# Ten mixer units of a two-layer hybrid step, worked in a different order

## The chip, the cores and the metric

The kernel runs on one core of one Trainium2 chip. The metric is device time in microseconds (us), as the median of the runs shown. One further execution was recorded by the hardware profiler, and every row below comes from it. Engine names: PE is TensorE (matmuls and transposes), PEld its weight loads, DVE is VectorE, ACT is ScalarE, POOL is GpSimd, and SP is SyncE, which issues every transfer of this kernel in one queue.

## What is computed

Two layers, each over 640 tokens: 512 latent ones and 128 prompt ones, with a model width of 1024. Cut to what matters here, a layer is:

```python
h = rmsnorm(x, g_norm1) * (1 + m[1]) + m[0]
z = h @ w_in                       # q, k, v of three mixers, and three gates
oa = diff_attention(qa, ka, va)    # (softmax(q1 k1) - lam softmax(q2 k2)) v, then a per-head norm
ob = gqa_attention(qb, kb, vb)     # q and k normalised per head and rotated first
oc = neighbourhood_attention(...)  # a window of the grid plus context, with a bias
x = x + m[2] * (sum(gate_i * (o_i @ w_branch_i)) @ w_out)
x = x + m[5] * (relu(rmsnorm(x, g_norm2) ... @ w1) ** 2 @ w2)
```

The latent tokens read their own keys and 128 cached context keys. The prompt tokens read only their own keys, and their keys and values are outputs too.

## The kernel before

The program is recorded as a list of operations, each with its engine, its operands and an estimated length. A planner (`Plan.schedule`) then goes through the list and decides, engine by engine, the order in which the operations are issued: whenever an engine is free it takes, among the operations that are ready by its estimate, the one with the lowest place in the list (moved a little by `EVAC` and `FILL`, one number for each kind of unit). So the order in which the program is written is a priority, and the order on each engine is fixed before the run. On the chip each engine works through its own fixed order and waits wherever the next operation isn't ready.

A layer's first stage, the mixers, is cut into `NU = 10` units of 384 columns of `w_in`. `kind(u)` gives the kind: units 0 to 3 are differential (A, one head pair each), 4 and 5 are grouped-query (B, four query heads each), and 6 to 9 are neighbourhood (C, two heads each). In this text A2 or B5 means the kind and the unit's number. The loop over the units, L1307, does three things for each:

- `project` (L924): for each of five tiles of 128 tokens, 24 matmuls of 128x384 into one of two PSUM banks. The weight blocks come from a stream (`ws`), in the order in which the host has packed them (`_stream`, L1571); each is split by ACT and POOL into a high and a low part ahead of use. There is room for ten blocks, and one unit needs eight.
- `evacuate` (L932), per tile: for A, DVE and POOL rotate q and k. For B there is a chain ahead of that: ACT squares, DVE sums, POOL takes the power -1/2 (a tensor_tensor on 128x5), and DVE scales five heads (five operations on 128x64). For C nothing is rotated. Then all kinds are split into high and low parts, transposed by PE through a single bank, and copied out.
- `jobs` (L1095): the attention itself. A has one job, B five (four heads and the prompt), C three. A job has two or three stages: scores, maximum, exponential and row scaling; then transposes of the rows and the product with v; for A also a norm over the head and a store. `step(i)` (L1300) writes one stage of each of three jobs into the list, so a unit's attention stands in the list just behind its projection and ahead of the next unit's. A row is 640 wide in A and B and 384 wide in C, and POOL scales it (L305).

The unit's number also picks its buffers: two places each for q, k and the prompt's k, three for v (L856). After the ten units come the gates and branch products, the output projection and the MLP. Those begin with gate products that need none of the mixers' outputs, so PE can take them while the last jobs run; each writes two of six PSUM banks.

Of the kernel before, what the change touches and what calls it, by code (L numbers as in the profile page):

```python
# [25 lines left out]
NU = 10  # L26
# [16 lines left out]
PRE = 2  # L43
LAG = 3
ORDER = (0, 1, 4, 2, 3)
LAM_INIT = [0.8 - 0.6 * math.exp(-0.3 * l) for l in range(DEPTH)]


# [9 lines left out]
class Plan:  # L58
# [16 lines left out]
    def __init__(self, nc):  # L75
        self.nc = nc
        self.ops = []
        self.writer = {}
        self.readers = {}
        self.bias = 0  # L80
        self.views = {}
# [380 lines left out]
def hybrid_plan(pl, a, mf, mr, view, psm, xspill, ospill):  # L462
# [44 lines left out]
    class Banks:  # L507
        def __init__(self, ids, w=1):
            self.ids, self.w, self.i = ids, w, 0
# [311 lines left out]
    def kind(u):  # L821
        return "A" if u < 4 else ("B" if u < 6 else "C")
# [29 lines left out]
            self.kp = [u1b[:, 1536:1792], u1b[:, 1792:2048]]  # L852

    class Unit:
        def __init__(self, l, u, ph):
            self.l, self.u, self.k, self.p = l, u, kind(u), ph  # L856
            q, kk, v, kp = ph.q[u % 2], ph.kk[u % 2], ph.v[u % 3], ph.kp[u % 2]
            self.kp = kp.rearrange("p (h k) -> p h k", h=2)
            self.qall = q.rearrange("p (f t) -> p f t", f=4)
            if self.k == "B":  # L860
                self.q = self.qall
                self.kk = kk.rearrange("p (h k) -> p h k", h=2)
                self.v = v[:, :6 * P].rearrange("p (c d) -> p c d", c=6)
            elif self.k == "A":
                self.q = q.rearrange("p (h s t) -> p h s t", h=2, s=2)
                self.kk = kk.rearrange("p (h k) -> p h k", h=2)
                self.v = v.rearrange("p (c s d) -> p c s d", c=6, s=2)
            else:
                self.q = q.rearrange("p (h s t) -> p h s t", h=2, s=2)
                self.kk = kk.rearrange("p (h k) -> p h k", h=2)  # L870
                self.v = v.rearrange("p (c h d) -> p c h d", c=6, h=2)
# [228 lines left out]
        def job_A(self):  # L1100
# [43 lines left out]
            pl.ptt(ssum, ssum, mhalf[:, :5], ALU.pow)  # L1144
            pl.pts(ssum, ssum, 1.0 - LAM_INIT[l], 0.0, ALU.mult, ALU.add)
            tt(on, on, ssum.unsqueeze(2).to_broadcast([P, 5, P]), ALU.mult)
# [130 lines left out]
    first = first_norm(Turns([u0[:, i * D:(i + 1) * D] for i in range(6)] + [wms.get(), wms.get()]), Bump(u1, 0, UNIT1A), u1c[:, :D])  # L1277
    first_z = {t: psm[:, b, :UW] for t, b in zip(ORDER, (2, 0, 1, 3, 7))}
    W = []
    for k in first:  # L1280
        W.append(ws.get(UW, 1))
        for t in ORDER:
            Unit.summand(None, first_z[t], W, t, k)
# [7 lines left out]
    for l in range(DEPTH):  # L1291
        ts(nlam[:, l:l + 1], nlam[:, l:l + 1], 1.0, -LAM_INIT[l], ALU.mult, ALU.add)

    for l in range(DEPTH):
        last = l == DEPTH - 1
        ph = Phase1()
# [7 lines left out]
                    next(jobs[j], None)  # L1304

        n = 0
        for u in range(NU):  # L1307
            un = Unit(l, u, ph)
            un.cached()
            if l == 0 and u == 0:  # L1310
                for t in ORDER:
                    un.evacuate(first_z[t], t)
            else:
                ws.hold = ws.cur
                W = [ws.get(UW, 1) for _ in range(KT)]
                ws.hold = None
                for t in ORDER:
                    un.project(W, t)
            for job in un.jobs():
                jobs.append(job)  # L1320
                step(n)
                n += 1
# [247 lines left out]
def _stream(i):  # L1570
    parts, pairs = [], []  # L1571
    for l in range(DEPTH):
        w_in = i["w_in"][l]
        for u in range(NU):
            parts.append(_kmajor(w_in[:, _unit_cols(u)], 0, UW))
        for b, n in enumerate(("w_branch_a", "w_branch_b", "w_branch_c")):
            for d in range(KT):
# [26 lines left out]
    out, at, np_ = [], 0, 0  # L1604
# [113 lines left out]
```

## Time and profile before

| what | value |
|---|---|
| median of 3 runs (lowest, highest) | 2405.42 us (2403.06, 2407.76) |
| profiled execution: its time | 2407.02 us |
| profiled execution: its span | 2405.1 us |
| mean granted TensorE clock | 0.989 |
| PE busy, weight loads busy | 2331.6 us (97%), 2262.4 us (94%) |
| DVE busy | 1825.6 us (76%) |
| ACT busy | 1215.3 us (51%) |
| POOL busy | 447.9 us (19%) |
| transfers | 245.39 MB, mean 102 GB/s |

The span runs from the first to the last instruction; 1.9 us of the profiled execution's time lie around it. Busy time counts an engine's own instructions, so an engine that waits isn't busy. The two layers have their mixers at about 84 to 500 us and 1215 to 1665 us of the span.

### The profile page before, as it was taken

The page shows a single profiled execution, that of the slowest core. Times are in us where ns is not written, and L with a number is a line of the kernel's source. Part 1 is how long each engine was busy: PE and PEld are TensorE (multiplying, and loading weights), DVE is VectorE, ACT ScalarE, POOL GpSimd, SP SyncE. Part 2 cuts the span into 40 slices and gives each one's busy share as a digit, 9 for nine tenths or more (in the row PEclk, how much of TensorE's full clock was granted, in tenths as well). Part 3 has the DMA queues.
Part 4 walks back from the last instruction along what each step waited for, and adds up shares of the span by engine and source line. Part 5 has one row for each costly group of instructions (what it writes and reads, how often), then busy time and mean ns, then how long its engine had stood idle before and what let it go on. Part 6 is the DMA issues. An engine that isn't in the chain of part 4 may idle for free. (4 is left out here: it accounts for less than half of the span.)

```text
span 2405.1 us, 42038 instructions
## 1 busy us (share of the span) xinstructions
PE 2331.6 (97%) x15484; PEld 2262.4 (94%) x15484; DVE 1825.6 (76%) x4002; ACT 1215.3 (51%) x2826; POOL 447.9 (19%) x528
## 2 busy tenths in 40 slices
PE   7899999999999999999999999999999999999997
PEld 5898999999999999999989998999999999999997
DVE  6878778789836999877777887777983677777776
ACT  4556677642232735444476567765232363544442
POOL 4535533310000000000034455431000000000000
PEclk8999999999999999999999999999999999999998
DMA  6211112476422244332241112136662222223322
GB/s 243 84 49 59 58 44 68 137 238 213 151 79 65 77 140 132 106 85 79 77 130 51 57 48 61 56 104 219 203 214 74 83 59 73 81 80 84 82 73 67
DMA packets 104754, 245.39 MB, mean 102 GB/s; under 512 B 12770, under 2 KB 24546, under 8 KB 103524
## 3 DMA queue, kind: packets, MB, share of 16 engines
q1 hardware_dynamic: 104548, 242.71, 32.9%
q8 instruction: 122, 2.00, 0.4%
q14 instruction: 84, 0.69, 0.1%
HBM read 225.62 MB, written 17.04 MB: 101 GB/s over the span
## 5 line engine op out<-in xcount | busy, mean ns | idle before, releaser
L245 PE MATMUL psm<-mr 128*128 128x384 f32 (+2 forms) x10784 | 1807.1, 319 | 20.1 <-ACT mr L262 8.1
L245 PEld LDWEIGHTS psm<-mr 128*128 128x128 f32 x10784 | 1657.8, 189 | 29.7 <-ACT mr L262 10.2
L262 ACT ACTIVATE mr<-mf 128x384 fp32r<-128x384 f32 (+4 forms) x956 | 471.5, 515 | 675.3 <-PE psm L245 589.1
L267 DVE TENSOR_TENSOR mr<-mf,mr 128x384 fp32r<-128x384 f32 (+5 forms) x795 | 438.4, 564 | 170.8 <-ACT mr L262 165.7
L311 POOL TENSOR_TENSOR mf<-mf 128x256 f32<-128x256 f32 (+3 forms) x93 | 90.4, 973 | 1236.0 <-DVE mf L267 1215.9
L280 DVE SCALAR_TENSOR_TENSOR mf<-psm,mf 128x256 f32<-128x256 f32 (+2 forms) x580 | 209.8, 407 | 107.2 <-PE psm L245 97.6
L262 ACT ACTIVATE mf<-mf 128x320 f32<-128x320 f32 (+6 forms) x409 | 191.9, 491 | 100.5 <-DVE mf L267 48.1
L305 POOL TENSOR_SCALAR mf<-mf 128x640 f32<-128x640 f32 (+3 forms) x236 | 145.4, 620 | 353.0 <-DVE mf L267 289.8
L294 DVE CUSTOM_DVE_ANT_0 psm<-mf,U1B 128x1024 f32<-128x1024 f32 x160 | 198.4, 1240 | 10.4 <-DMA mf<-wmod 9.5
L311 POOL TENSOR_TENSOR mr<-mf,mr 128x384 fp32r<-128x384 f32 (+1 forms) x169 | 189.4, 1142 | 55.1 <-ACT mr L262 54.4
L262 ACT ACTIVATE mf<-psm,mf 128x640 f32<-128x640 f32 (+3 forms) x256 | 162.6, 643 | 65.7 <-DVE mf L267 48.3
L267 DVE TENSOR_REDUCE mf<-psm 128x1 f32<-128x640 f32 (+2 forms) x212 | 148.4, 704 | 39.1 <-PE psm L245 33.5
L245 PE MATMUL psm<-U,mr 128*128 128x320 f32 (+1 forms) x1110 | 174.9, 305 | 0.6 <-ACT mr L262 0.5
L245 PEld LDWEIGHTS psm<-U,mr 128*128 128x128 f32 x1110 | 163.7, 189 | 1.2 <-ACT mr L262 0.6
L267 DVE TENSOR_TENSOR mr<-psm,mr 128x512 fp32r<-128x512 f32 (+2 forms) x252 | 141.1, 579 | 24.5 <-ACT mr L262 22.0
L245 PE MATMUL psm<-U1A,mr 128*128 128x256 f32 (+2 forms) x814 | 152.9, 309 | 0.0
L262 ACT ACTIVATE mr<-psm 128x512 fp32r<-128x512 f32 (+2 forms) x252 | 123.7, 513 | 53.5 <-PE psm L248 45.9
L267 DVE TENSOR_TENSOR mf<-mf 128x320 f32<-128x320 f32 (+8 forms) x261 | 134.2, 522 | 8.5 <-POOL mf L305 5.9
L245 PEld LDWEIGHTS psm<-U1A,mr 128*128 128x128 f32 x814 | 132.2, 188 | 0.0
L267 DVE TENSOR_TENSOR mf<-psm,mf 128x128 f32<-128x128 f32 (+5 forms) x248 | 93.0, 391 | 43.8 <-ACT mf L262 23.4
L248 PE MATMUL psm<-mf 128*128 128x128 f32 x752 | 120.2, 276 | 4.6 <-DVE mr L267 2.6
L262 ACT ACTIVATE mf<-psm 128x320 f32<-128x320 f32 (+7 forms) x188 | 76.3, 410 | 75.1 <-PE psm L245 71.0
(95 smaller groups left out, 1714.4 us busy)
## 6 DMA issues: line engine op xcount, KB each, us to landing
mf<-w SPq DMA_DIRECT2D x232, 384.0 KB, 3.2
mf<-wmod SPq DMA_DIRECT2D x84, 512.0 KB, 3.8
mf<-w SPq DMA_DIRECT2D x156, 256.0 KB, 2.7
U1C<-w SPq DMA_DIRECT2D x48, 256.0 KB, 2.7
mf<-bias SPq DMA_DIRECT2D x8, 1024.0 KB, 5.4
U<-wmod SPq DMA_DIRECT2D x12, 512.0 KB, 6.1
mf<-x SPq DMA_DIRECT2D x16, 320.0 KB, 7.0
ospill<-mf SPq DMA_DIRECT2D x16, 256.0 KB, 2.6
```

The costliest lines, as they stand in the source:

```text
L245: self.add("PE", d, lambda R: self.nc.tensor.matmul(R(out), R(lhsT), R(rhs), start=start, stop=stop), [out], [lhsT, rhs])
L248: self.add("PE", 55 if in_.dtype == F32R else 108, lambda R: self.nc.tensor.transpose(R(out), R(in_), ident), [out], [in_, ident])
L262: self.add("ACT", d, lambda R: self.nc.scalar.activation(R(out), R(in_), func, **kw), outs, ins)
L267: self.add("DVE", d, lambda R: getattr(self.nc.vector, name)(R(out), *map(R, ins), *args, **kw), [out] + list(extra), list(ins) + [x for x ...
L280: self.add("DVE", d, lambda R: self.nc.vector.scalar_tensor_tensor(R(out), R(a), s, R(b), op0, op1), [out], [a, b] + ([s] if hasattr(s, "a ...
L294: self.add("DVE", d, lambda R: self.nc.vector.tensor_tensor_reduce(out=R(out), in0=R(a), in1=R(b), scale=1.0, scalar=0.0, op0=ALU.mult, op ...
L305: self.add("POOL", d, lambda R: self.nc.gpsimd.tensor_scalar(R(out), R(a), s1, s2, op0, op1), [out], [a] + [s for s in (s1, s2) if hasattr ...
L311: self.add("POOL", d, lambda R: self.nc.gpsimd.tensor_tensor(R(out), R(a), R(b), op), [out], [a, b])
```

## The change

The loop over the units, and the host code that packs the weight stream, take the units in the order of a new table: A0, C6, A1, B4, C7, A2, C8, B5, A3, C9 in place of A0 to A3, B4, B5, C6 to C9. A unit's buffers are picked by its place in that order and no longer by its number. No operation is added or removed, and no size changes.

```diff
@@ -43,6 +43,7 @@
 ORDER = (0, 1, 4, 2, 3)
+UNITS = (0, 6, 1, 4, 7, 2, 8, 5, 3, 9)
@@ -852,9 +853,9 @@
     class Unit:
-        def __init__(self, l, u, ph):
+        def __init__(self, l, u, ph, n):
             self.l, self.u, self.k, self.p = l, u, kind(u), ph
-            q, kk, v, kp = ph.q[u % 2], ph.kk[u % 2], ph.v[u % 3], ph.kp[u % 2]
+            q, kk, v, kp = ph.q[n % 2], ph.kk[n % 2], ph.v[n % 3], ph.kp[n % 2]
@@ -1304,8 +1305,8 @@
         n = 0
-        for u in range(NU):
-            un = Unit(l, u, ph)
+        for at, u in enumerate(UNITS):
+            un = Unit(l, u, ph, at)
             un.cached()
@@ -1571,7 +1572,7 @@
         w_in = i["w_in"][l]
-        for u in range(NU):
+        for u in UNITS:
             parts.append(_kmajor(w_in[:, _unit_cols(u)], 0, UW))
```

The planner then issues the same operations in another order on every engine. Three places follow, all in the first layer; source lines are one higher after the change.

DVE, the third tile of B5's evacuation. The rows on 128x64 are its five head scalings; 128x512 on `mr` is the low part of a job's transposed rows, TENSOR_REDUCE from `psm` to 128x1 is a row maximum of a job. Before:

```order
L280 SCALAR_TENSOR_TENSOR mf<-psm,mf 128x64 x2
L267 TENSOR_TENSOR mr<-psm,mr 128x512 x2
L267 TENSOR_REDUCE mf<-psm 128x1
L280 SCALAR_TENSOR_TENSOR mf<-psm,mf 128x64
L267 TENSOR_TENSOR mr<-psm,mr 128x512
L267 CAST U1C_93_650<-psm 128x2x128
L267 RECIPROCAL mf<-mf 128x1
L280 SCALAR_TENSOR_TENSOR mf<-psm,mf 128x64 x2
```

After:

```order
L281 SCALAR_TENSOR_TENSOR mf<-psm,mf 128x64 x4
L268 TENSOR_TENSOR mf<-psm,mf 128x128
L281 SCALAR_TENSOR_TENSOR mf<-psm,mf 128x64
L268 CAST U1C_93_648<-psm 128x2x128
L268 TENSOR_TENSOR mr<-mf,mr 128x4x64
L268 TENSOR_TENSOR U_4_78_510<-mf,U_4_78_510 128x128
L268 TENSOR_REDUCE mf<-mf 128x5
L268 TENSOR_TENSOR mr<-mf,mr 128x128
```

Before, the five scalings stood in three pieces, with maxima and splits of B4's and A3's jobs between them. After, they stand in two pieces, and what follows are copies and splits of evacuations, of A2's job and of A3's cached keys.

POOL, beside a grouped unit's evacuation. TENSOR_TENSOR 128x5 is the power -1/2, with a TENSOR_SCALAR 128x5 ahead of it; `mr` 128x384 is the low part of a weight block of the next unit; TENSOR_SCALAR 128x640 scales a row of an A or B job, and 128x384 a row of a C job. Before, B4's evacuation, while B5's weights are made ready:

```order
L305 TENSOR_SCALAR mf<-mf 128x640
L311 TENSOR_TENSOR mr<-mf,mr 128x384 x4
L311 TENSOR_TENSOR mf<-mf 128x320
L305 TENSOR_SCALAR mf<-mf 128x640
L305 TENSOR_SCALAR mf<-mf 128x5
L311 TENSOR_TENSOR mr<-mf,mr 128x384
L311 TENSOR_TENSOR mf<-mf 128x5
L311 TENSOR_TENSOR mr<-mf,mr 128x384
L305 TENSOR_SCALAR mf<-mf 128x128
L311 TENSOR_TENSOR mr<-mf,mr 128x384
L305 TENSOR_SCALAR mf<-mf 128x5
L311 TENSOR_TENSOR mf<-mf 128x5
```

After, B5's evacuation, while A3's weights are made ready:

```order
L306 TENSOR_SCALAR mf<-mf 128x384
L306 TENSOR_SCALAR mf<-mf 128x5
L312 TENSOR_TENSOR mf<-mf 128x5
L306 TENSOR_SCALAR mf<-mf 128x5
L312 TENSOR_TENSOR mr<-mf,mr 128x384
L306 TENSOR_SCALAR mf<-mf 128x5
L312 TENSOR_TENSOR mr<-mf,mr 128x384
L312 TENSOR_TENSOR mf<-mf 128x5
L306 TENSOR_SCALAR mf<-mf 128x384
L312 TENSOR_TENSOR mr<-mf,mr 128x384 x2
L306 TENSOR_SCALAR mf<-mf 128x5
L312 TENSOR_TENSOR mr<-mf,mr 128x384
```

Weight blocks stand between the powers in both. The rows scaled there were 640 wide, of A3, and are 384 wide, of C8; behind the piece before came the evacuation of a second grouped unit, and behind the piece after comes a differential one.

POOL, the end of the mixer stage. Before, with C8 and C9 last:

```order
L305 TENSOR_SCALAR mf<-mf 128x384 x2
L311 TENSOR_TENSOR mr<-mf,mr 128x384 x6
L305 TENSOR_SCALAR mf<-mf 128x384
L311 TENSOR_TENSOR mr<-mf,mr 128x384
L305 TENSOR_SCALAR mf<-mf 128x384 x2
L305 TENSOR_SCALAR mf<-mf 128x128 x2
L305 TENSOR_SCALAR mf<-mf 128x384 x5
L305 TENSOR_SCALAR mf<-mf 128x128 x2
L305 TENSOR_SCALAR mf<-mf 128x384 x8
```

After, with B5, A3 and C9 last (128x256 is the rotation of A3's last tile, the 128x5 rows are A3's norm over its head):

```order
L312 TENSOR_TENSOR mf<-mf 128x256
L312 TENSOR_TENSOR mr<-mf,mr 128x384
L306 TENSOR_SCALAR mf<-mf 128x640 x11
L306 TENSOR_SCALAR mf<-mf 128x128
L306 TENSOR_SCALAR mf<-mf 128x384 x6
L306 TENSOR_SCALAR mf<-mf 128x5
L312 TENSOR_TENSOR mf<-mf 128x5
L306 TENSOR_SCALAR mf<-mf 128x5
L306 TENSOR_SCALAR mf<-mf 128x384
L306 TENSOR_SCALAR mf<-mf 128x128 x2
L306 TENSOR_SCALAR mf<-mf 128x384
```

Before, the last rows are those of two neighbourhood units. After, eleven rows of 640 columns of B5 and A3 stand there behind the last weight block, and A3's norm stands among C9's rows.

## Rows read from the trace of the kernel before

**Rows 1.** The page: busy time, share of the span and instructions of each engine; and TensorE's granted clock in the 40 slices of the span, in tenths.

```profile
PE 2331.6 (97%) x15484; PEld 2262.4 (94%) x15484; DVE 1825.6 (76%) x4002; ACT 1215.3 (51%) x2826; POOL 447.9 (19%) x528
...
PEclk8999999999999999999999999999999999999998
```

**Rows 2.** Busy time of each engine in four long stretches: the first layer's mixers, the rest of that layer, the second layer's mixers, the rest. Columns: stretch in us, its length, then PE, PEld, DVE, ACT and POOL busy (instructions), granted clock, DMA share, GB/s.

```profile
84.00:500.00 416.00, 401.51 (x2613) 378.81 (x2612) 320.02 (x807) 277.06 (x732) 173.88 (x220) 0.99 0.25 79
500.00:1215.00 715.00, 713.02 (x4870) 711.99 (x4869) 558.21 (x1134) 297.75 (x608) 15.99 (x14) 1.00 0.38 114
1215.00:1665.00 450.00, 432.77 (x2793) 404.32 (x2792) 347.37 (x864) 304.54 (x796) 196.69 (x239) 1.00 0.28 88
1665.00:2405.00 740.00, 725.06 (x4935) 723.33 (x4933) 540.65 (x1104) 300.59 (x612) 17.87 (x16) 0.99 0.34 100
```

**Rows 3.** SP's queue in order of time: the stores of a unit's prompt tile (`newz`), which come at the third of its five tiles. These are A3, B4, B5 and C6 of the first layer. Columns: start us, length us, what.

```profile
177.39 0.34 SPq L317 DMA_DIRECT2D newz<-mf  x1
...
225.09 0.34 SPq L317 DMA_DIRECT2D newz<-mf  x1
...
273.05 0.34 SPq L317 DMA_DIRECT2D newz<-mf  x1
...
313.33 0.34 SPq L317 DMA_DIRECT2D newz<-mf  x1
```

**Rows 4.** Busy time in stretches between such stores, columns as in rows 2. The first seven are the first layer: to A3's store, to B4's, to B5's, to C6's, to C7's, to C9's, and the end of the stage. The other seven are the same of the second layer.

```profile
84.00:177.00 93.00, 89.65 (x573) 85.86 (x572) 74.05 (x182) 55.88 (x152) 39.43 (x44) 0.98 0.17 53
177.00:225.00 48.00, 45.30 (x300) 42.71 (x299) 37.76 (x97) 29.19 (x79) 22.50 (x29) 1.00 0.17 54
225.00:273.00 48.00, 43.40 (x278) 41.74 (x277) 38.58 (x105) 27.66 (x78) 26.79 (x33) 0.93 0.16 49
273.00:313.00 40.00, 38.47 (x258) 35.50 (x257) 32.56 (x81) 28.84 (x78) 22.07 (x29) 1.00 0.21 62
313.00:365.00 52.00, 51.18 (x332) 47.61 (x331) 36.02 (x81) 38.03 (x94) 20.53 (x26) 1.00 0.16 50
365.00:458.00 93.00, 91.93 (x601) 85.44 (x600) 73.12 (x195) 70.33 (x190) 36.45 (x51) 1.00 0.27 89
458.00:500.00 42.00, 41.58 (x284) 39.94 (x283) 27.94 (x70) 27.14 (x68) 6.11 (x10) 1.00 0.70 227
1250.00:1344.00 94.00, 90.78 (x585) 86.55 (x585) 72.09 (x167) 56.80 (x150) 45.87 (x50) 1.00 0.23 71
1344.00:1391.00 47.00, 44.66 (x296) 42.24 (x295) 37.89 (x99) 28.90 (x79) 23.39 (x27) 1.00 0.17 55
1391.00:1436.00 45.00, 42.74 (x278) 40.62 (x278) 38.46 (x104) 27.59 (x77) 27.09 (x33) 0.96 0.16 52
1436.00:1477.00 41.00, 37.95 (x258) 35.65 (x257) 31.88 (x80) 28.48 (x78) 23.44 (x30) 1.00 0.20 60
1477.00:1535.00 58.00, 57.25 (x365) 52.46 (x365) 41.60 (x91) 42.27 (x103) 21.32 (x28) 1.00 0.16 50
1535.00:1621.00 86.00, 85.07 (x551) 78.61 (x550) 65.76 (x182) 63.04 (x176) 34.84 (x49) 1.00 0.29 93
1621.00:1665.00 44.00, 43.37 (x298) 41.23 (x297) 30.54 (x75) 28.88 (x72) 7.21 (x10) 1.00 0.67 216
```

**Rows 5.** What PE waited for from 177 to 313 us, longest first: us in total, times, longest.

```profile
PE psm L245 <- POOL mr L311: 2.8, 2, 2.3
PE psm L245 <- DVE mf L280: 1.9, 2, 0.9
PE psm L248 <- DVE mr L267: 1.5, 3, 0.8
```

**Rows 6.** The same from 313 to 458 us.

```profile
PE psm L248 <- DVE mf L267: 0.8, 1, 0.8
PE psm L248 <- ACT mr L262: 0.3, 1, 0.3
```

**Rows 7.** POOL in order of time, while B4 is evacuated. Columns: start us, length us, what, and in brackets the idle time ahead of it and what ended it.

```profile
235.50 0.88 POOL L311 TENSOR_TENSOR mf<-mf 128x320 f32<-128x320 f32 x1 [0.49 <-DVE mf L267]
236.36 1.88 POOL L305 TENSOR_SCALAR mf<-mf 128x640 f32<-128x640 f32 x2
238.32 1.05 POOL L311 TENSOR_TENSOR mr<-mf,mr 128x384 fp32r<-128x384 f32 x1
```

**Rows 8.** PE in order of time over the same stretch and a little on.

```profile
232.97 4.11 PE L245 MATMUL psm<-mr 128*128 128x384 f32 x22 [0.94 <-DVE mf L280]
239.42 0.62 PE L245 MATMUL psm<-mr 128*128 128x384 f32 x2 [2.34 <-POOL mr L311]
...
243.07 2.44 PE L245 MATMUL psm<-mr 128*128 128x384 f32 x7
```

**Rows 9.** SP's queue: the stores of A2's and of A3's outputs (`ospill`) in the first layer.

```profile
264.63 0.33 SPq L317 DMA_DIRECT2D ospill<-mf  x1
...
288.52 0.34 SPq L317 DMA_DIRECT2D ospill<-mf  x1
```

**Rows 10.** PE between those stores: the 40 products of A3's job with v (128x256).

```profile
270.75 1.31 PE L245 MATMUL psm<-U,mr 128*128 128x256 f32 x9
...
272.22 1.58 PE L245 MATMUL psm<-U,mr 128*128 128x256 f32 x11
...
273.93 2.56 PE L245 MATMUL psm<-U,mr 128*128 128x256 f32 x20
```

## The prediction, made before the run

> **What bounds the kernel now.** I read the page first. PE is busy for 2331.6 of 2405.1 us, and its granted clock is nine tenths or more of full speed in all slices but the first and the last [rows 1]. So PE sets the end, and the change can give back only time in which PE stands still or runs at its lower clock. The long stretches show where that is: from 500 to 1215 us PE is idle for 2.0 us, while in the two mixer stages it is idle for 14.5 and 17.2 us [rows 2]. The change touches these stages alone, so no more than some 30 us of idle time and a few us of clock are at stake, in 2405.
>
> Next I cut the stages into steps at the stores of each unit's prompt tile, which mark how far the units have come; the first layer has A3's at 177.39 us, B4's at 225.09, B5's at 273.05 and C6's at 313.33 [rows 3]. In each step I take as lost PE's idle time, plus the length times what the mean granted clock lacks to 1.00 (a share s of the time at 1.2 GHz in place of 2.4 lowers the mean by s/2 and loses s/2 of the work). From [rows 4], both layers together:
>
> - differential beside differential (84 to 177, 1250 to 1344): idle 3.35 + 3.22, clock 0.02 x 93 = 1.9; 8.4 us of 187, 4.5%.
> - the first grouped unit, B4's projection beside differential jobs (177 to 225, 1344 to 1391): 2.70 + 2.34 = 5.0 us of 95, 5.3%.
> - the second, B5's projection with B4's evacuation and jobs beside it (225 to 273, 1391 to 1436): idle 4.60 + 2.26, clock 0.07 x 48 + 0.04 x 45 = 5.2; 12.1 us of 93, 13%.
> - from B5 to C6 (273 to 313, 1436 to 1477): 1.53 + 3.05 = 4.6 us of 81, 5.7%.
> - grouped jobs beside a neighbourhood projection (313 to 365, 1477 to 1535): 0.82 + 0.75 = 1.6 us of 110, 1.4%.
> - neighbourhood units (365 to 458, 1535 to 1621): 1.07 + 0.93 = 2.0 us of 179, 1.1%.
> - the end of the stage (458 to 500, 1621 to 1665): 0.42 + 0.63 = 1.1 us of 86.
>
> Together 34.8 us. The reader is to see that the loss isn't spread: the step between the two grouped units loses a third of it in 11% of the time. What PE waits for there is POOL's low parts of weight blocks (2.8 us) and DVE's head scalings (1.9 us) [rows 5]; from 313 to 458 us the longest group of waits is 0.8 us [rows 6]. One of them in detail: POOL works through a rotation of B4 and scalings of A3's rows until 238.32 and only then takes the low part of B5's next block, 1.05 us [rows 7]; PE, idle for 2.34 us, starts again at 239.42, and soon after, seven matmuls take 2.44 us [rows 8], 349 ns each, the lower of the two clock levels.
>
> **The change part by part.** Nothing is added or removed on any engine, so the sum is one of losses alone. The program ahead of the second unit is the same, and so are the branch stage and the MLP.
>
> First, no grouped unit now stands beside another. B4 is evacuated beside A1's jobs as it was beside A3's, and its term stays at 5.0. B5 is evacuated beside C8's jobs. The trace has no such step. Its bounds are the neighbourhood rate (1.1% of 93 us, 1.0 us) and the rate that it has now (12.1 us). I take the nearest step in which one grouped unit is evacuated beside jobs of another kind, B4's 5.3%, which is 4.9 us: **-7.2 us**.
>
> Second, B5's jobs now run beside A3's evacuation, where they ran beside C7's. That step isn't in the trace either. It lies between the 1.4% of grouped jobs beside a neighbourhood unit (no loss, 0) and the 13% of grouped beside grouped (11.6% of one 55 us step in each layer, +12.8 us). An evacuation of A has the rotation of B's and not its chain of squares, sums and powers, so I take the differential rate, 4.5%: 3.1% x 55 x 2 = **+3.4 us**.
>
> Third, differential and neighbourhood units alternate, 366 us in which 10.4 us are lost now. If each unit kept its own loss whatever stands beside it, this would be 0. If all went at the neighbourhood rate it would be 1.1% x 366 = 4.0, a gain of 6.4; if all went at the differential rate, 16.5, a loss of 6.1. For a gain speaks that ACT has 55.88 of 93 us to do beside A and 70.33 of 93 beside C, so the two kinds leave room to each other; against it, that DVE, for which PE waits, has 74.05 and 73.12 us in the same two steps [rows 4] and is not evened out by the change. I take half the gain: **-3.2 us**.
>
> Fourth, the moved transfers. The first bias load keeps its place behind the first weights, and the other three no longer follow one upon another; the stream has the same blocks in the order in which they are used. PE's waits in [rows 5, 6] name POOL, DVE and ACT and no transfer, so I take 0. If a load were late, the whole of POOL's and ACT's work on weight blocks would be behind it on PE's path; but what is loaded for each unit, and the two places for it, are as before.
>
> Fifth, the end of the stage. Before, two neighbourhood units close it; now C9's jobs share it with those of A3 and with the last of B5. The cover is the gate products of the next stage: they use six banks, two for each, so three can go ahead, some 144 matmuls. At 715 us for 4870 matmuls [rows 2] they are about 21 us of work. That is enough for 1.1 us lost in 86 now; I take 0 and give the uncovered case below as a rival.
>
> The sum is -7.2 + 3.4 - 3.2 = -7.0 us. The profiled execution took 2407.0 us, of which 2405.1 are the span; it would take 2400.0. The median of the runs is 2405.4, and I forecast **2398.4 us**. A measurement of this kernel can tell about 0.2%, 4.8 us, from no change, so the forecast is just a gain that can be seen.
>
> The weight loads tell another story. By PEld's busy time in [rows 4], A beside A is idle for 14.6 of 187 us (7.8%), neighbourhood units for 15.0 of 179 (8.4%), the first grouped step for 10.1 of 95 (10.6%), the second for 10.6 of 93 (11.4%), grouped jobs beside C for 9.9 of 110 (9.0%). By these shares the first term is -0.8, the second -1.3 (7.8% in place of 9.0%), the third within 1.1: about -2 us, and 2403.3. The Trainium skill, "Perfetto Trace Analysis", section "Identifying the Most-Contended Engine", says that matmul busy time is a poor measure because matmuls are pipelined, and that the busy share of weight loads is to be used. By that rule the steps differ far less than I have taken, and it speaks against this change; I follow the rows of waits and of the clock, since both are time in which PE certainly did nothing or half.
>
> **The rivals.** *The whole stage runs at the rate of its best steps.* If the trouble is like beside like, every step falls to 1.2%: 10.0 us of 831 in place of 34.8, -24.8 us, 2380.6. For it speaks that grouped jobs lose only 1.4% where a neighbourhood unit is projected beside them; against it, DVE's even share. The Trainium skill, "Perfetto Trace Analysis", section "Optimization Strategy", says that interleaving stretches whose busiest engine differs may help; here DVE is busy for 80% in the first step of the list and 79% in the neighbourhood step, so the rows don't show such stretches. Chance 0.15.
>
> *The loss moves along with the units.* Each evacuation costs what it costs, and B5 beside C8's three short jobs finds as little cover as beside B4. The first and third terms are then nil and the rest small: 0 to -2 us, 2404 to 2405.4. The weight loads' shares speak for it. Chance 0.23.
>
> *The end of the stage is uncovered*, on the other side. A differential unit ends on a long chain: in the first layer A2's output is stored at 264.63 us and A3's at 288.52, 23.9 us apart [rows 9], and PE's products with v in between take 1.31 + 1.58 + 2.56 = 5.5 us [rows 10]. That chain ran beside a projection; now it runs after the last one, together with rows of B5 that POOL still has to scale. If half of the 18.4 us in which PE needs other work isn't covered, each layer loses 9.2 us: -7.0 + 18.4 = +11.4, 2416.8. It decides once the 21 us of gate products are used up before A3's products are ready. Against it: the cover is nearly as long as the chain, and C9's jobs lie beside it. Chance 0.15.
>
> **How the numbers follow.** The forecast has 0.47, with a spread of some 4 us about it. Faster by over 0.2%, below 2400.6: the first rival and nearly four fifths of the forecast, 0.52. Slower, above 2410.2: the last rival, and 0.04 for a first term of nil with the second at its upper end, 0.19. The rest, 0.29, is within 0.2%. The range is 2384 to 2412: the lower end leaves out the tip of the first rival (about 0.08), the upper end most of the last (about 0.1). Taken alone the forecast has 2392 to 2405.
>
> **What would show it.** In the changed trace, the step in which B5 is projected should lose about 2.5 us in each layer, at a full clock, with no wait of over 2 us for POOL's low parts. The step in which A3 is evacuated beside B5's jobs should lose about 2.5 us. Steps that alternate A and C should lie between 1.1% and 4.5%. The last 45 us of each stage should stay under 1 us idle; a row of PE waiting for DVE's or ACT's splits of A3 there would be the last rival's. The prediction is wrong if B5's step still loses 4 us or more, if the clock falls in new places, or if the idle time of the stages falls under 12 us in all.

## The result, and the profile after

The changed kernel takes **2437.7 us** (median of 4 runs, 2437.4 to 2438.8) beside 2405.7 us for the kernel before on the same chip (2403.1 to 2407.8). The ratio is 1.0136, 95% interval 1.0122 to 1.0150: slower by 32 us, where 7 us less was forecast, and above the range of 2384 to 2412. The profiled execution's span is 2436.0 us, 30.9 longer.

The page after, the rows that answer to [rows 1]:

```profile
PE 2346.0 (96%) x15484; PEld 2263.0 (93%) x15484; DVE 1817.1 (75%) x4002; ACT 1213.0 (50%) x2826; POOL 446.4 (18%) x528
...
PEclk8899999999999999999999999999999999999998
```

The same instructions, but PE counts 14.4 us more busy time. PEld counts 0.6 more, so PEld's idle time has grown by 30.3 us, as much as the span. This is the first thing to see: PE's idle time grew by 16.5 us only, half of what was lost, because a matmul that stands by itself counts as busy for longer than one in a stream (two score products of 128x384 alone take 0.62 us, 0.31 each, and 24 products of that size in a row take 4.42, 0.18 each; both rows stand below). The Trainium skill, "Perfetto Trace Analysis", section "Identifying the Most-Contended Engine", says that the busy share of matmuls is not a good measure of how close a kernel comes to its limit, because pipelined PE instructions look smaller in the trace, and that the share of peak FLOPs and the busy share of weight loads are to be used. Here the trace agrees as far as the weight loads go: their idle time shows all of the loss.

Where the time went, in stretches that answer to [rows 2] and to the ends of [rows 4] (stretch, length, then busy PE, PEld, DVE, ACT, POOL, granted clock, DMA share, GB/s):

```profile
84.00:516.00 432.00, 410.00 (x2621) 380.10 (x2619) 318.25 (x808) 274.44 (x729) 176.07 (x220) 0.98 0.23 73
516.00:1231.00 715.00, 712.86 (x4865) 711.73 (x4866) 558.63 (x1134) 299.51 (x614) 17.04 (x14) 1.00 0.38 115
```

The 715 us behind the stage hold 4865 PE instructions, as they held 4870 before [rows 2]. The first layer's stage takes 432 us for 2621 where it took 416 for 2613. So the loss is in the mixer stages; the measure below puts it at 15.0 us in the first and 15.5 in the second.

Prompt stores of B4, B5, A3 and C9 in the first layer (SP's queue, as [rows 3]):

```profile
191.29 0.34 SPq L318 DMA_DIRECT2D newz<-mf  x1
...
361.68 0.34 SPq L318 DMA_DIRECT2D newz<-mf  x1
...
396.93 0.34 SPq L318 DMA_DIRECT2D newz<-mf  x1
...
446.53 0.34 SPq L318 DMA_DIRECT2D newz<-mf  x1
```

Steps between such stores, columns as above. First layer: to C6's store, to C7's, to B5's, to A3's, and the end behind C9's; second layer: to C7's, to B5's, to A3's, and the end.

```profile
84.00:111.00 27.00, 24.16 (x140) 22.66 (x139) 16.58 (x52) 14.36 (x43) 4.58 (x6) 0.85 0.13 39
...
191.00:231.00 40.00, 36.72 (x234) 33.99 (x233) 31.35 (x79) 23.82 (x68) 19.31 (x22) 0.96 0.19 59
...
321.00:362.00 41.00, 40.61 (x266) 38.40 (x266) 35.09 (x102) 27.29 (x79) 20.72 (x26) 1.00 0.26 83
362.00:397.00 35.00, 33.61 (x228) 31.62 (x227) 27.59 (x71) 23.31 (x66) 22.22 (x30) 1.00 0.22 72
...
447.00:516.00 69.00, 60.68 (x389) 54.82 (x387) 45.43 (x106) 37.41 (x97) 11.41 (x18) 0.98 0.38 127
```

```profile
1369.00:1408.00 39.00, 36.95 (x234) 34.09 (x234) 29.31 (x76) 23.75 (x65) 19.21 (x21) 0.96 0.19 60
...
1497.00:1544.00 47.00, 44.41 (x283) 41.14 (x283) 36.58 (x105) 28.43 (x81) 22.48 (x29) 1.00 0.24 74
1544.00:1577.00 33.00, 32.60 (x221) 30.45 (x220) 25.13 (x69) 23.58 (x67) 20.36 (x27) 1.00 0.24 74
...
1626.00:1696.00 70.00, 60.51 (x396) 54.34 (x395) 46.71 (x108) 37.48 (x97) 10.90 (x18) 1.00 0.36 117
```

The end, which lost 1.1 us in 86 before [rows 4], is idle for 8.3 and 9.5 us now. The step of B5, the subject of the first term, is idle for 0.4 and 2.6 us. PE's longest waits in the steps of B5 and A3, 321 to 397 us (us in total, times, longest), where [rows 5] had 2.8 us for POOL:

```profile
PE psm L249 <- DVE mf L268: 0.7, 2, 0.4
PE psm L246 <- DVE mf L281: 0.5, 1, 0.5
```

What PE did at the end of the first layer's stage, in order of time (rows with `psm<-mr` and 256 or 384 columns are gate products; `U` is A3's place for q and k, `U1C,U1A` that of B5 and then C9):

```profile
438.41 0.53 PE L246 MATMUL psm<-U1C,U1A 128*128 128x320 f32 x2
...
440.77 0.56 PE L246 MATMUL psm<-U 128*128 128x320 f32 x2 [0.25 <-ACT mf L263]
...
467.67 0.46 PE L246 MATMUL psm<-U 128*128 128x320 f32 x2
...
471.10 1.23 PE L246 MATMUL psm<-mr 128*128 128x256 f32 x9
472.57 0.33 PE L249 MATMUL psm<-mf 128*128 128x128 f32 x1 [0.24 <-DVE mf L281]
473.47 0.66 PE L249 MATMUL psm<-mf 128*128 128x128 f32 x4 [0.57 <-ACT mf L263]
474.61 0.62 PE L246 MATMUL psm<-U1C,U1A 128*128 128x384 f32 x2 [0.48 <-ACT mf L263]
...
476.47 0.59 PE L246 MATMUL psm<-U1C,U1A 128*128 128x384 f32 x2
...
482.30 1.38 PE L249 MATMUL psm<-mf 128*128 128x128 f32 x8 [0.96 <-DVE mf L268]
...
485.61 3.75 PE L246 MATMUL psm<-U,mr 128*128 128x256 f32 x20
...
493.47 4.42 PE L246 MATMUL psm<-mr 128*128 128x384 f32 x24
498.64 0.76 PE L249 MATMUL psm<-mf 128*128 128x128 f32 x5 [0.76 <-DVE mf L268]
499.95 0.97 PE L246 MATMUL psm<-mr 128*128 128x384 f32 x4 [0.54 <-ACT mf L263]
```

B5's last scores are at 438.41, A3's first at 440.77 and its last at 467.67, though A3's prompt tile was stored at 396.93. The gate products stop at 472.3 us and go on at 493.47: 72 of them had run (counted in the trace from 458.9 on), and 72 more follow before the stage ends. In these 21 us PE runs pieces of one to twenty matmuls; nine of the sixteen rows there begin with a wait of 0.2 to 1.0 us for a result of ACT or DVE.

What the gate products waited for can be read too. Neighbourhood units put their rows of scores into banks 3, 4 and 5 by turns, and the gate products take banks 0 to 5 in pairs; by this count the gate products of 493.47 need the bank of C9's sixth row, whose scores are at 476.47. These are DVE's maxima of the fifth and sixth row, and then ACT's rows:

```profile
478.11 1.00 DVE L268 TENSOR_REDUCE mf<-psm 128x1 f32<-128x384 f32 x2
```

```profile
489.04 0.63 ACT L263 ACTIVATE mf<-psm 128x128 f32<-128x128 f32 x2 [2.45 <-PE psm L246]
...
492.72 0.58 ACT L263 ACTIVATE mf<-psm,mf 128x384 f32<-128x384 f32 x1
...
499.23 0.58 ACT L263 ACTIVATE mf<-psm,mf 128x384 f32<-128x384 f32 x1 [4.19 <-PE psm L249]
```

The sixth row's maximum is there at 479.1, but its exponential comes at 492.72, behind the copies of A3's outputs (128x128), and the gate products start less than 0.2 us after it is done. The next ones, at 499.95, wait for ACT too, for the seventh row's exponential at 499.23. In the second layer it is the same: the sixth row's scores at 1657.71, its exponential at 1673.37, the gate products at 1674.11. So the banks that the gate products needed were taken by C9's rows, and these were held up behind A3. Whether a row buffer that A3 still had or only its place in ACT's fixed order kept the exponential back isn't shown; ACT stood idle for 2.45 us ahead of the first copies.

PE's longest waits at the end of the second layer's stage, 1640 to 1700 us (us in total, times, longest), are of the same kind:

```profile
PE psm L246 <- ACT mf L263: 3.3, 6, 0.9
PE psm L249 <- DVE mf L268: 3.0, 2, 2.1
```

**A measure for the experiments.** Since idle time shows only half, I count as lost, for each PE instruction, the time to the start of the next one less what the same form takes in a stream (medians of the starts in the traces: 0.174 us for 384 columns, 0.146 for 320, 0.117 for 256, 0.229 for 512, 0.108 and 0.062 for the two kinds of transposes). A unit's step runs from the first matmul of its projection to that of the next; the end runs from the last projection on. A0 of the first layer is projected ahead of its stage and has no step there. Lost us, first layer and second:

```
before  A1 3.0  A2 2.0  A3 7.5  B4 6.9  B5 10.0 C6 3.7  C7 2.9  C8 3.8  C9 4.6  end 1.4   sum 45.9
after   C6 9.1  A1 3.8  B4 5.6  C7 9.0  A2 3.1  C8 3.5  B5 3.7  A3 4.1  C9 3.7  end 15.3  sum 60.9
before  A0 9.4 A1 2.6 A2 3.3 A3 2.5 B4 5.8 B5 6.9 C6 6.3 C7 3.2 C8 4.3 C9 4.3  end 1.8    sum 50.5
after   A0 9.4 C6 4.5 A1 2.5 B4 3.5 C7 8.0 A2 3.8 C8 4.5 B5 5.6 A3 3.8 C9 4.3  end 16.1   sum 66.0
```

The sums differ by 30.5 us, so this measure accounts for the result. Of it, 28.2 us are the two ends; the steps ahead of them, taken together, lose 2.3 us more than before.

### The profile page after: what moved, and what is told of

Its sections match the earlier page's. It is cut to its first block, busy times and chain, and to the rows that moved or that the text cites. A ratio compares the mean times of both kernels' runs of the same rounds, so it can differ in the third digit from the quotient of the medians.

```text
span 2436.0 us, 41971 instructions
## 1 busy us (share of the span) xinstructions
PE 2346.0 (96%) x15484; PEld 2263.0 (93%) x15484; DVE 1817.1 (75%) x4002; ACT 1213.0 (50%) x2826; POOL 446.4 (18%) x528
## 4 chain that ended last, share of the span: by engine, by line
PE 83%; DVE 8%; ACT 4%; issue 2%; POOL 2%; DMA 0%; POOLq 0%; SPq 0%; DVEq 0%; ACTq 0%
PE psm L246 79%; PE psm L249 4%; DVE mf L268 3%; DVE mr L268 2%; ACT mf L263 2%; ACT mr L263 1%; DVE mf L281 1%; POOL mf L312 1%; POOL mr L312 1%; DVE U L268 1%; DVE U1C L295 1%; POOL mf L306 0%; ACT U L263 0%; DVE U1B L268 0%; ACT U1B L263 0%
## 5 line engine op out<-in xcount | busy, mean ns | idle before, releaser
L246 PEld LDWEIGHTS psm<-mr 128*128 128x128 f32 x10784 | 1655.9, 189 | 31.4 <-ACT mr L263 10.2
L268 DVE TENSOR_TENSOR mr<-mf,mr 128x384 fp32r<-128x384 f32 (+5 forms) x795 | 431.8, 556 | 170.8 <-ACT mr L263 166.8
L246 PE MATMUL psm<-U,mr 128*128 128x320 f32 (+1 forms) x1194 | 187.7, 304 | 3.3 <-DVE mf L268 2.0
L268 DVE TENSOR_REDUCE mf<-psm 128x1 f32<-128x640 f32 (+3 forms) x212 | 148.5, 704 | 56.8 <-PE psm L246 51.5
L246 PEld LDWEIGHTS psm<-U,mr 128*128 128x128 f32 x1194 | 175.0, 189 | 5.4 <-DVE mr L268 2.4
L249 PE MATMUL psm<-mf 128*128 128x128 f32 x752 | 125.8, 279 | 12.4 <-DVE mf L268 5.9
L249 PEld LDWEIGHTS psm<-mf 128*128 128x128 f32 x752 | 92.3, 143 | 26.0 <-DVE mf L268 7.5
```

What stands on the lines that cost most here:

```text
L246: self.add("PE", d, lambda R: self.nc.tensor.matmul(R(out), R(lhsT), R(rhs), start=start, stop=stop), [out], [lhsT, rhs])
L249: self.add("PE", 55 if in_.dtype == F32R else 108, lambda R: self.nc.tensor.transpose(R(out), R(in_), ident), [out], [in_, ident])
L268: self.add("DVE", d, lambda R: getattr(self.nc.vector, name)(R(out), *map(R, ins), *args, **kw), [out] + list(extra), list(ins) + [x for x ...
```

## The experiments

Each is the changed kernel with another order in `UNITS`, unless said otherwise. "Lost" is the sum over both layers by the measure above (before 96.4, after 126.9).

| kernel | order | us | ratio to before (95%) | lost |
|---|---|---|---|---|
| e1 | A0 C6 A1 B4 C7 A2 B5 A3 C8 C9 | 2427.1 | 1.0092 (1.0077 to 1.0107) | 118.9 |
| e2 | A0 A1 A2 B4 C6 C7 C8 B5 A3 C9 | 2443.9 | 1.0161 (1.0146 to 1.0176) | 133.1 |
| e3 | A0 A1 A2 B4 A3 B5 C6 C7 C8 C9 | 2429.1 | 1.0099 (1.0084 to 1.0114) | 117.4 |
| e4 | A0 A1 C6 B4 C7 A2 C8 B5 A3 C9 | 2437.9 | 1.0135 (1.0118 to 1.0152) | 127.4 |
| e5 | A0 C6 A1 B4 C7 A2 C8 A3 B5 C9 | 2417.9 | 1.0053 (1.0040 to 1.0066) | 108.1 |
| e6 | A0 A1 A2 A3 B4 C6 B5 C7 C8 C9 | 2415.1 | 1.0041 (1.0028 to 1.0053) | 104.9 |
| e7 | A0 C6 A1 C7 A2 A3 B4 B5 C8 C9 | 2414.2 | 1.0035 (1.0022 to 1.0047) | 103.1 |
| e8 | A0 A1 B4 C6 A2 A3 C7 B5 C8 C9 | 2405.6 | 0.9997 (0.9988 to 1.0006) | 95.2 |
| e9 | as e3, values placed otherwise | 2408.5 | 1.0011 (1.0002 to 1.0020) | 97.1 |
| e10 | A0 C6 A1 B4 B5 C7 A2 C8 A3 C9 | 2420.1 | 1.0059 (1.0047 to 1.0072) | 110.5 |
| e11 | A0 A1 A2 B4 B5 C6 C7 A3 C8 C9 | 2407.2 | 1.0010 (1.0001 to 1.0019) | 96.7 |
| e12 | A0 C6 A1 B4 C7 A2 A3 B5 C8 C9 | 2417.6 | 1.0049 (1.0037 to 1.0061) | 107.9 |
| e13 | as before, other PSUM banks | 2403.7 | 0.9988 (0.9979 to 0.9996) | 93.3 |

**Is it the end, and is it the order of the end?** e1 puts C8 back to the end; e2 has the change's end behind a front of like units; e4 undoes only the exchange of A1 and C6.

```diff
-UNITS = (0, 6, 1, 4, 7, 2, 8, 5, 3, 9)
+UNITS = (0, 6, 1, 4, 7, 2, 5, 3, 8, 9)   # e1
+UNITS = (0, 1, 2, 4, 6, 7, 8, 5, 3, 9)   # e2
+UNITS = (0, 1, 6, 4, 7, 2, 8, 5, 3, 9)   # e4
```

> The changed order with the end of the old one: A0, C6, A1, B4, C7, A2, B5, A3, C8, C9, so B5 and A3 stand one place earlier and two neighbourhood units close the stage. The theory of the uncovered end (the 12 us that each layer loses more in its last 45 to 60 us come from A3's chain and B5's rows left over behind the last projection) expects the end to fall back to about 1 us idle and the time to about 2413 us, 24 below the changed kernel. The rival (mixing costs everywhere and the end only shows it) expects 2430 us or more.

> The kernel before with only its end changed: A0, A1, A2, B4, C6, C7, C8, B5, A3, C9. The two grouped units are far apart, too. The theory of the uncovered end expects about 24 us more than the kernel before, less what the grouped units gain by standing apart (0 to 7): 2422 to 2430 us, with 8 us or more idle in the last 60 us of each layer's stage. The rival expects 2398 to 2408 us, as the start and the middle are those of the kernel before.

> The changed order with A1 ahead of C6, so that the second unit is a differential one as before: A0, A1, C6, B4, C7, A2, C8, B5, A3, C9. If C6 in second place costs the first layer its start (from 90 to 120 us the changed kernel has 3.1 us idle and a granted clock of 0.89, the kernel before 0.6 us and 1.00), the time is 5 to 6 us below the changed kernel, 2432 us, and the end still loses. If the start was made up for later, it is 2436 to 2439 us.

e1's end loses 2.5 us in each layer in place of 15.3 and 16.1, but its C9 step loses 11.1 and 12.0 in place of 3.7 and 4.3, so only 10.6 us come back: a miss of both expectations. e2 is slower than the change and 14 us above even the range of the theory, which named the place and not the size: its end loses 22.4 and 25.8 us. So this end is expensive with either front. In e4 the step of C6 falls from 9.1 to 3.5 us in the first layer, and the end rises to 21.8 and 21.3: the time is the same (the second expectation), and the first step's loss isn't a cost that can be taken off by itself. Why the ends of e2 and e4 are longer than the change's wasn't tried.

**The first term alone, and the place for values.** e3 moves only A3, between the grouped units.

```diff
-UNITS = (0, 6, 1, 4, 7, 2, 8, 5, 3, 9)
+UNITS = (0, 1, 2, 4, 3, 5, 6, 7, 8, 9)   # e3
```

> The kernel before with A3 between the two grouped units and nothing else moved: A0, A1, A2, B4, A3, B5, C6 to C9. The first term of the prediction by itself: 2398.5 us (7.2 us less), with the step in which B5 is projected losing 5 us in both layers together in place of 12. The rival, that a loss moves along with its unit, expects 2403 to 2408 us.

24 us slower than before, outside both expectations. B5's step did fall, from 10.0 and 6.9 to 3.2 and 4.7. But C6's, the next, lost 16.8 and 15.2. PE in e3, from 302 to 322 us, and a row of ACT:

```profile
309.30 1.13 PE L246 MATMUL psm<-U1C,U1A 128*128 128x320 f32 x3
310.23 0.46 PE L249 MATMUL psm<-mr 128*128 128x128 f32 x2
311.60 0.48 PE L249 MATMUL psm<-mf 128*128 128x128 f32 x1 [0.92 <-DVE mf L281]
312.50 1.12 PE L249 MATMUL psm<-mf 128*128 128x128 f32 x4 [0.42 <-ACT mf L263]
315.03 1.11 PE L249 MATMUL psm<-mf 128*128 128x128 f32 x4 [1.41 <-DVE mr L268]
...
317.71 3.96 PE L246 MATMUL psm<-mr,U 128*128 128x512 f32 x10
```

```profile
321.25 0.57 ACT L263 ACTIVATE U<-psm 64x128 fp32r<-64x128 f32 x2 [1.06 <-PE psm L246]
```

From 302.5 to 322 us no row of 128x384 stands in that view: C6's projection has stopped. The ten products of 128x512 are the last of B4, and right behind them ACT writes C6's values (64x128 into `U`). The three places for values go by turns (`n % 3`), so C6, three units behind B4, has B4's place, and with two PSUM banks for projections it can't go on until B4's last products have read that place. A grouped unit fills only half of its place; e9 gives B5 the other half of B4's and C6 the place that this leaves free, without any more memory:

```diff
 UNITS = (0, 1, 2, 4, 3, 5, 6, 7, 8, 9)
+VAT = (0, 1, 2, 0, 1, 0, 2, 1, 0, 2)
+VHALF = (0, 0, 0, 0, 0, 1, 0, 0, 0, 0)
-            q, kk, v, kp = ph.q[n % 2], ph.kk[n % 2], ph.v[n % 3], ph.kp[n % 2]
+            q, kk, v, kp = ph.q[n % 2], ph.kk[n % 2], ph.v[VAT[n]], ph.kp[n % 2]
+                v = v[:, VHALF[n] * 6 * P:]       # for kind B
```

> The order of e3 (A3 between B4 and B5) with one thing more: where the values of each unit lie. The three places for values go round by turns, so C6, three units behind B4, has B4's place and cannot be evacuated until B4's last products have read it; a grouped unit fills only half a place. Here B5 gets the second half of B4's place, and C6 the whole place that is then free; no memory is added. Theory (the 16.8 and 15.2 us lost in C6's step are projection work that cannot go on because C6's evacuation waits for B4's values): C6's step falls to 8 us or less in each layer and the time by 12 us or more, to 2408 to 2416. Rival (A3's job behind B4's five is what holds PE up, the place of the values is not): C6's step keeps 12 us or more, and the time stays at 2424 to 2430.

The same 20 us in e3 and in e9 (columns as above):

```profile
302.00:322.00 20.00, 14.76 (x61) 10.88 (x60) 11.73 (x29) 10.34 (x29) 3.84 (x5) 0.66 0.02 7
```

```profile
302.00:322.00 20.00, 19.83 (x128) 18.29 (x128) 13.62 (x38) 14.43 (x39) 5.04 (x7) 1.00 0.05 18
```

C6's step loses 3.6 and 6.9 us, and the time falls by 20.6 us, to 2408.5, as the theory expected: the reused place was e3's cost. A3 still stands behind B4 in e9, so that alone costs little here. e1's C9 stands three units behind B5 in the same way, and a row there reads like the one above; no run tried it.

```profile
451.54 0.57 ACT L263 ACTIVATE U<-psm 64x128 fp32r<-64x128 f32 x2 [1.44 <-PE psm L246]
```

A place that is used again is not a cost by itself: before the change C7 and C8 stand three behind the grouped units, and after it C8 stands three behind B4. ACT waits of 0.6 us and more ahead of such a write, ended by a product of 128x512, are in e1 and e3 in both layers, once in e2, and in no other of the fifteen traces. In the change itself no unit stands three behind B5, so its end must have another cause.

**The cause of the end.** e5 exchanges B5 and A3. e10 moves B5 away and leaves C8, A3, C9. e12 takes e5 and puts C8 to the end.

```diff
-UNITS = (0, 6, 1, 4, 7, 2, 8, 5, 3, 9)
+UNITS = (0, 6, 1, 4, 7, 2, 8, 3, 5, 9)   # e5
+UNITS = (0, 6, 1, 4, 5, 7, 2, 8, 3, 9)   # e10
+UNITS = (0, 6, 1, 4, 7, 2, 3, 5, 8, 9)   # e12
```

> The changed order with one pair exchanged: A3 now goes ahead of B5 (0, 6, 1, 4, 7, 2, 8, 3, 5, 9); C9 is the last unit as in the change. Theory: the loss of 12 to 17 us per layer comes where a differential unit stands directly behind a grouped one, since A3's single job must wait in the order of score banks and row buffers until the five jobs of B5 have been through, and whatever comes two steps later finds nothing to cover that chain. With A3 ahead of B5 no such pair is left near the end: the end of each stage should lose no more than 5 us in place of 15 and 16, and the time be about 2414 to 2420. Rival (the end is short of cover because a grouped unit stands second to last, whatever its neighbours): the end still loses 12 us or more per layer, and the time stays at 2432 to 2440.

> The changed order with B5 moved from the eighth place to the fifth, behind B4 (0, 6, 1, 4, 5, 7, 2, 8, 3, 9); C8, A3 and C9 still close the stage. Theory (the end of the stage is long because A3's job comes behind B5's five): the end loses 6 us or less per layer in place of 15 and 16, and the time is 2412 to 2424. Rival (A3's own chain so near the end is what isn't covered, with or without a grouped unit ahead of it): the end still loses 12 us or more per layer, 2430 or more.

> The order of e5 with C8 moved from ahead of A3 to behind B5 (0, 6, 1, 4, 7, 2, 3, 5, 8, 9), so that two neighbourhood units close the stage as before the change. If what is left of the end's loss in e5 (6.6 and 6.0 us, against 1.4 and 1.8 before) comes from there being one neighbourhood unit at the end and not two: the end loses 3 us or less per layer, and the time is 2405 to 2412. If the mixed front of the stage is what still costs: 2414 to 2420.

The first layer behind the last projection, after, and then in e5:

```profile
459.00:484.00 25.00, 21.02 (x136) 18.32 (x134) 20.41 (x50) 13.56 (x37) 4.52 (x7) 1.00 0.24 75
484.00:509.00 25.00, 22.48 (x142) 21.07 (x143) 10.96 (x26) 10.97 (x32) 4.92 (x9) 0.93 0.38 135
```

```profile
449.00:477.00 28.00, 27.22 (x180) 24.61 (x179) 21.75 (x47) 18.79 (x42) 7.10 (x8) 1.00 0.26 82
477.00:505.00 28.00, 26.07 (x171) 23.73 (x170) 19.34 (x46) 17.04 (x42) 5.78 (x11) 1.00 0.59 208
```

5.6 instructions per us become 6.3. e5's ends lose 6.6 and 6.0 us in place of 15.3 and 16.1, a little over the 5 us that the theory allowed, and 19.8 of the 32 us are gone with one exchange, as it had it. In e10 the ends lose 8.0 and 10.1, between the two expectations, and the time falls by 17.5 us. So both units count: without B5 in front, A3 second to last still leaves 18.1 us at the ends, where 3.2 were lost before and 31.4 after the change, so that about half of the end's loss needs the grouped unit right ahead of the differential one. Of what is left in e5, 11.7 us by the measure, 9.4 are at its ends. In e12 the first layer's end keeps 6.1, the second's falls to 3.0, but B5's step then loses 8.7 and 7.9 in place of 5.0 and 6.4: no gain. The time is in the second expectation's range, but its reason, the mixed front, is only a part: of the 11.5 us that e12 loses more than before, 5.9 are still at the ends.

The traces show what these ends have in common. The longest gap between gate products comes after exactly 72 of them (us from start to start, first layer and second): 21.4 and 21.1 after the change, 29.1 and 30.8 in e2, 29.0 and 27.3 in e4, 14.8 and 9.2 in e5, 6.5 and 9.9 in e10, 8.0 in the first layer of e12. In the second layer of e12 and in all other traces, whose ends lose little, no gap is over 3 us. So the cover that goes ahead has the same size in each; what the order changes is how long the next bank stays taken. In the change, e2, e4 and e10 the gap ends within 0.1 us of ACT's last work on an exponential of a neighbourhood row; in e5 and e12 that wasn't read.

**The first and third terms where nothing differential follows.** e6 has only C6 moved between the grouped units; e7 mixes only A and C.

```diff
-UNITS = (0, 6, 1, 4, 7, 2, 8, 5, 3, 9)
+UNITS = (0, 1, 2, 3, 4, 6, 5, 7, 8, 9)   # e6
+UNITS = (0, 6, 1, 7, 2, 3, 4, 5, 8, 9)   # e7
```

> The order before with only C6 moved between the two grouped units (0, 1, 2, 3, 4, 6, 5, 7, 8, 9): no differential unit stands behind a grouped one. This is the first term of the prediction by itself. Theory (the first term is right where nothing differential follows): B5's step falls from 10.0 and 6.9 us lost to 3 to 4, C6's beside B4's jobs stays at 4 to 6, and the time is 2395 to 2401. Rival (the loss moves along with the units, or a short neighbourhood projection is too little cover for B4's five jobs): 2403 to 2412.

> Only the third term: C6 and C7 go between A0, A1 and A2, then A3, B4, B5, C8, C9 as before (0, 6, 1, 7, 2, 3, 4, 5, 8, 9). If alternating differential and neighbourhood units gave half the gain that the third term reckons with: 2400 to 2404. Theory now, from the trace of the change, where C6's step behind A0 loses 9.1 us in the first layer and 4.5 in the second against 2.5 to 3.0 for A1's there before: no gain, 2406 to 2414.

e6 is 9.2 us slower than before, outside both expectations. B5's step falls to 3.9 and 1.9, but C6's behind B4 now loses 8.9 and 7.9, and C7's behind B5 6.6 and 7.1. The step behind B4 in e6 (C6's projection, to hold against [rows 4], where B5 is projected from 225 to 273 us):

```profile
234.00:283.00 49.00, 46.28 (x301) 43.96 (x301) 32.04 (x82) 27.44 (x77) 18.84 (x23) 0.93 0.15 47
```

PE idle for 2.7 us and the clock at 0.93, though it is a neighbourhood unit that is projected there: what I had put down to two grouped units side by side belongs largely to the step behind B4, whichever unit comes. Over all fifteen traces and both layers that step loses 6.4 to 10.0 us in 25 of 30 cases; the exceptions are e4 (4.9 and 4.7), e7's first layer (3.4, with B5 there), e8's second (3.9) and e10's second (5.5), and they are not explained. e7 is 8.3 us slower, at the upper edge of what was expected. C6 behind A0 loses 9.1 us in the first layer where A1 lost 3.0; but as B5's step falls from 10.0 to 3.4, that layer as a whole loses only some 1 us more than before, and the rest is lost in the second layer, in the steps from B5 on. PE's longest waits behind A0, the same in e7 as after the change:

```profile
PE psm L249 <- DVE U1B L268: 1.6, 1, 1.6
PE psm L249 <- ACT U L263: 0.7, 2, 0.5
```

These are A0's own transposes; why they come late wasn't tried.

**Orders made by the theory, and the banks.**

```diff
-UNITS = (0, 6, 1, 4, 7, 2, 8, 5, 3, 9)
+UNITS = (0, 1, 4, 6, 2, 3, 7, 5, 8, 9)   # e8
+UNITS = (0, 1, 2, 4, 5, 6, 7, 3, 8, 9)   # e11
```

> An order made by the theory: the grouped units far apart, each with a neighbourhood unit behind it before a differential one comes, and two neighbourhood units at the end (0, 1, 4, 6, 2, 3, 7, 5, 8, 9). If only a differential unit directly behind a grouped one, and a short end, cost time, this is faster than before: 2392 to 2402. If mixing costs time wherever it is done, it is at 2410 to 2430.

> The two grouped units together and two neighbourhood units behind them, then A3 third from the end: (0, 1, 2, 4, 5, 6, 7, 3, 8, 9). No differential unit stands behind a grouped one, the first four steps are as before, and two neighbourhood units close the stage. By the theory this costs nothing against before: 2398 to 2408. If a differential unit late in the stage costs time by itself: 2412 or more.

Both cost nothing that counts (2405.6 and 2407.2), and neither gains. e11 is as expected; e8 falls between its two expectations: leaving out the orders that cost time did not yet make it faster. An order can avoid the loss of 32 us, but none of these gave the 7 us of the forecast. e13 keeps the order before and changes banks:

```diff
-    zb, tz, sb1, tb_ = Banks((0, 1)), psm[:, 2], Banks((3, 4, 5)), Banks((6, 7))
+    zb, tz, sb1, tb_ = Banks((0, 1)), psm[:, 2], Banks((3, 4)), Banks((5, 6, 7))
-            return (psm[:, 3:5], psm[:, 3:6:2], psm[:, 4:6])[(self.i - 1) % 3]
+            return psm[:, 3:5]
```

> The order before, with other places in PSUM: the rows of scores of differential and grouped units always take banks 3 and 4 (before, three pairs out of 3, 4 and 5 in turn), neighbourhood scores take 3 and 4 by turns, and the jobs' transposes and products get three banks, 5 to 7, where they had 6 and 7. If rows of scores go one after another anyway, since any two pairs out of three banks share one, the second pair is worth little and the third bank for transposes gives more: 2392 to 2402, faster than both kernels. If a row's scores do run ahead in the bank that is free: 2410 to 2425.

2403.7 us, the one kernel faster than before by more than its interval, by 0.12% (0.04 to 0.21%), between the two expectations. It changes the banks of scores and of transposes at once, so it doesn't say whether rows of scores are serial on their banks. That A3's scores start right behind B5's last is read from the rows; whether the score banks or the row buffers (the places for rows behind the exponential) hold them back stays open.

## Why the prediction was wrong

- **What bounds the kernel** was right: PE, and only the mixer stages changed. But "no more than some 30 us of idle time and a few us of clock are at stake" bounds a gain, not a loss, and it counted PE's idle time. By weight loads, [rows 4] already showed every step but the end 8 to 12% short; I worked that out for most of them and set it aside. It was the better measure.
- **First term (-7.2).** In its own place it came true: by the same reckoning B5's step loses 0.4 and 2.6 us, 3.0 in both layers, where 4.9 was forecast. But the step behind B4 (C7's) loses 3.3 + 1.6 (idle and clock) in the first layer and 2.1 + 1.6 in the second, 8.5 us, and I had no term for it. e6 shows it with little else changed: the loss of the second step moves to the steps behind both grouped units, 9.2 us slower in place of 7.2 faster. That is the mechanism of the rival "the loss moves along with the units", though not its size, 0 to -2 us.
- **Second term (+3.4).** A3's step loses 1.4 and 0.4 us, less than reckoned. But B5's jobs reach beyond it, into the end.
- **Third term (-3.2).** e7 gives +8.3 and no gain anywhere in the alternating steps that counts: those of A0 to A3, C6 and C7 lose 5.6 us more than before in the first layer, where C6 behind A0 alone loses 6.1 more than A1 did, and 0.9 less in the second. The rest of e7's loss lies behind these steps.
- **Fourth (0).** Right as far as it went: no wait for a transfer stands among the longest. But it counted two places only for what a unit brings, "as before", and overlooked those for values, which are three: which unit takes whose place depends on the order. It cost the change itself nothing that shows, and e3 20.6 us.
- **Fifth (0), the step that failed.** "Three can go ahead, some 144 matmuls" was wrong: 72 went ahead, then none for 21 us in each layer, because the next banks were held by C9's rows, the first of them until 493.3 us. So the loss that this term put at 0 was 13.9 and 14.3 us. And 23.9 us, the distance between two stores in [rows 9], isn't the length of A3's chain: its first score is at 440.77 and its output is stored at

```profile
500.76 0.32 SPq L318 DMA_DIRECT2D ospill<-mf  x1
```

  which is 60.0 us later, with B5's last products and C9's scores among its own. Before the change the same stretch took 92.9 us (A3's first score at 195.59, its output at 288.52), but all of that lay beside projections. The last rival had the place and the mechanism, with 9.2 us per layer in place of 13.9 and 14.3. Its chance of 0.15 was too low, since the 18.4 us "in which PE needs other work" stood beside a cover counted at twice what could run.
- **What would show it** named 1 us idle in the last 45 us as what the end should stay under, and that row decided: 8.3 and 9.5 us. A second sign came too: the clock fell in a new place, to 0.85 in C6's step of the first layer. B5's step stayed under its 4 us in each layer.

## What to carry over

Before reordering, list what each step leaves unfinished, and not only what it costs: work whose results are consumed two steps later is paid for wherever the cover ends, which here is the end of the stage. Count the cover in buffers that are free at that moment, and work out for every reused buffer which unit had it before under the new order. Where many small dependent matmuls may take the place of streams, reckon by weight loads or by instructions per microsecond, since busy time hid half of the loss here.

## What the runs showed that I had not expected

The same 15484 PE instructions were busy for 2331.6 us before and 2346.0 after, while their weight loads took 2262.4 and 2263.0. In e3 the granted clock fell to 0.66 over 20 us in which PE ran 61 instructions, and stayed at 1.00 in e9 with 128 in the same 20 us. PE's longest wait in that stretch of e3 is 1.41 us, and the ten products of 128x512 at its end take 3.96 us, 0.40 each, where a stream takes 0.23: here the stall was paid twice, once as waiting and once as slow matmuls.
